# A state-space mixer: silu as one activation, exponentials together, transposes later, decay differences as a biased relu on ACT

## The chip, the cores and the metric

The kernel runs on one core of a Trainium2 chip. The metric is the device time of that core for one launch, in microseconds (us), the median of the runs. The engines are named as in the profile: PE (TensorE, matrix products), PEld (its weight loads), DVE (VectorE), ACT (ScalarE), POOL (GpSimd), and SP, which issues most of the transfers.

## What is computed

The reference is a trunk of two layers over 512 positions of width 1024. The even layer has pooling and chunked attention; the odd layer has a Mamba-2 mixer; each is followed by a mixture of experts. The change touches the odd layer's mixer alone:

```python
zxbcdt = h @ w_in
z, xbc, dt = jnp.split(zxbcdt, [SSM_D_INNER, SSM_D_INNER + SSM_CONV_DIM], axis=-1)
conv = xp[:, 0:s] * conv_w[0]
for tap in range(1, SSM_D_CONV):
    conv = conv + xp[:, tap:tap + s] * conv_w[tap]
xbc = jax.nn.silu(conv + conv_b)
xs, Bm, Cm = jnp.split(xbc, [SSM_D_INNER, SSM_D_INNER + G * N], axis=-1)
...
seg = jnp.exp(jnp.where(tril, a_cs[..., :, None] - a_cs[..., None, :], -jnp.inf))
cb = jnp.einsum('bclgn,bcsgn->bcgls', Cm, Bm)
y_diag = jnp.einsum('bcgls,bcgrls,bcsgrp->bclgrp', cb, seg, x_dt)
...
y = y_diag + y_off + xs * D_skip
g = (y * jax.nn.silu(z)).reshape(b, s, G, SSM_D_INNER // G)
g = g * lax.rsqrt(jnp.mean(g * g, axis=-1, keepdims=True) + EPS)
return (g.reshape(b, s, SSM_D_INNER) * norm_w) @ w_out
```

## The kernel before

The mixer is `odd_mixer` (L1455). It works in 8 head groups g, each with 128 channels of b and of c and two chunks of 128 of x and of z. The positions (512) lie along the free axis, and the scan is done in four position chunks cq of 128. A loop over g = 0 to 8 (L1727) does the projections and most of group g together with the last steps of group g-1.

The steps, with the names of the code and of the trace:

- A projection (`Dense.next`, L436, tiles pdb, pdc, pdx, pdz) is 24 products of 128x512 for 128 channels, since weights and input are split in a high and a low part. There are six per group, in the order b, c, x0, x1, z0, z1. The splits of the weights (L111 on ACT, L112 on DVE or POOL) run ahead.
- `conv` (L1580) reads a projection: a scaled copy with bias on ACT (L1584), three taps on DVE (L1587), Tanh on ACT (L1590), and the product (tanh + 1) times the value on DVE (L1591). The weights are halved beforehand, so this is the silu.
- `cbt` (L1594): c times b per chunk and its mask (cbm), and b transposed (btk).
- `decay` (L1614), for each cq: a row of cumulative decays comes by DMA to all partitions (lb, two buffers); DVE takes the difference to the own decay and its minimum with 0, four heads in turn (L1620, tile ms, three buffers); ACT takes Exp (L1622); POOL (even cq) or DVE (odd cq) multiplies by cbm (L1623).
- `xtok` (L1626): PE transposes x0 and x1 (L1637, pxd); DVE multiplies by the step size (xdt, L1640); POOL makes xw for the first three chunks (L1643).
- `states` (L1645): three products of xw and btk (pst, L1651), summed into prev on ACT and DVE (L1654 to L1659).
- `ymm` (L1661), for each cq: the diagonal products pyd of ms and xdt (L1670) and the products pyo of prev and c (L1674).
- `zgate` (L1677): Tanh of the projection on ACT (L1680), its product on DVE (L1681).
- `assemble` (L1683), for each of the two x chunks: yy and yt on DVE (L1686, L1689), their sum on POOL (L1691), the gate on DVE into gT (L1692), squares on ACT (L1695, L1698) and their sum gsum on POOL.
- `gnorm` (L1701), after every second group for two groups at once: sums over partitions on PE (pgn, L1705), variance gv on DVE (L1708), Ln and Exp on ACT (L1710, L1711), three DVE steps, broadcast to all partitions on POOL (gb, L1718), and gT times it on DVE (L1721).

The short-lived rows (tanh results, yt, squares, gv, gy, gb) share one ring of buffers under the tag "tmp", NTMP of them; a new one waits until the last reader of the buffer's holder is done.

Two other things stand in the same stretch. The modulation of the layer's second half is a product of one vector with a weight matrix of 1024 x 2048, done on DVE as a running sum, one instruction of 128x2048 for each 128 rows (L202 and L204, tile ada); OFILL says how many of these steps are put after each group. And at the end `out_proj` (tiles so) multiplies by w_out.

The order of the code is not the order on the engines. A scheduler orders each engine's instructions at build time by dependences and its own estimates, each engine then runs its list in that order, and waits are put in where they are needed. Exceptions can be pinned by hand.

Of the kernel before, what the change touches and what calls it, by code (L numbers as in the profile page):

```python
# [9 lines left out]
F32 = mybir.dt.float32  # L10
# [10 lines left out]
P = 128  # L21
T = 512
NT = 4
# [35 lines left out]
HEAD = 1  # L59
NTMP = 3  # L60
TAIL = 2
# [15 lines left out]
def trunk_kernel(ctx, tc, x, c, ada_w, ada_b, norm1_w, norm2_w, mix_w_in, pool_w, pool_scale,  # L77
# [1377 lines left out]
    def odd_mixer(layer, prev):  # L1455
        with ExitStack() as es:
# [25 lines left out]
            with ExitStack() as es2:  # L1482
# [94 lines left out]
                def tmp(name):  # L1577
                    return gp.tile([P, T], F32, tag="tmp", name=name, bufs=NTMP)

                def conv(kind, ch, bufs, between=None):  # L1580

                    p = dense.next(between)
                    a = gp.tile([P, T], F32, tag=f"cv{kind}", name=f"cv{kind}{ch}", bufs=bufs)
                    S.activation(a, p, AF.Identity, bias=cb[:, ch:ch + 1], scale=cw[:, 3, ch:ch + 1])  # L1584
                    for tap in (2, 1, 0):
                        sh = 3 - tap
                        V.scalar_tensor_tensor(a[:, sh:], p[:, :T - sh], cw[:, tap, ch:ch + 1], a[:, sh:], op0=ALU.mult,  # L1587
                                               op1=ALU.add)
                    t = tmp(f"cvt{ch}")
                    S.activation(t, a, AF.Tanh)  # L1590
                    V.scalar_tensor_tensor(a, t, 1.0, a, op0=ALU.add, op1=ALU.mult)  # L1591
                    return a
# [21 lines left out]
                def decay(g, cq):  # L1614

                    lb = gp.tile([P, 4, P], F32, tag="lb", name=f"lb{g}{cq}", bufs=2)
                    SP.dma_start(lb, dap(acd, (32 * cq + 4 * g) * P, [[0, P], [1, 4 * P]]))
                    ms = gp.tile([P, 4, P], F32, tag="ms", name=f"ms{g}{cq}", bufs=3)
                    for h in range(4):
                        V.tensor_scalar(ms[:, h, :], lb[:, h, :], acs[:, cq, 4 * g + h:4 * g + h + 1], 0.0,  # L1620
                                        op0=ALU.subtract, op1=ALU.min)
                    S.activation(ms, ms, AF.Exp)  # L1622
                    (V if cq % 2 else GP).tensor_mul(ms, ms, gs[g]["cbm"][:, cq, None, :].to_broadcast([P, 4, P]))  # L1623
                    gs[g]["ms", cq] = ms

# [51 lines left out]
                def zgate(g, q):  # L1677
                    pz = dense.next()
                    z = gs[g]["z", q] = gp.tile([P, T], F32, tag="zt", name=f"zt{g}{q}", bufs=2)
                    S.activation(z, pz, AF.Tanh, scale=0.5)  # L1680
                    V.scalar_tensor_tensor(z, z, 1.0, pz, op0=ALU.add, op1=ALU.mult)  # L1681

                def assemble(g, q):  # L1683
# [7 lines left out]
                    GP.tensor_add(y[:, P:], y[:, P:], t[:, P:])  # L1691
                    V.tensor_mul(gT[2 * g + q], y, d["z", q])  # L1692
                    if q == 0:
# [7 lines left out]
                def gnorm(g0):  # L1701
# [5 lines left out]
                    v = tmp(f"gv{g0}")  # L1707
                    V.tensor_scalar(v, p, 1.0 / 1024, EPS, op0=ALU.mult, op1=ALU.add)  # L1708
                    y = tmp(f"gy{g0}")
                    S.activation(y, v, AF.Ln)  # L1710
                    S.activation(y, y, AF.Exp, scale=-0.5)  # L1711
                    t = tmp(f"gt{g0}")
                    V.tensor_mul(t, y, y)
                    V.scalar_tensor_tensor(t, t, -0.25, v, op0=ALU.mult, op1=ALU.mult)
                    V.scalar_tensor_tensor(y, t, 0.75, y, op0=ALU.add, op1=ALU.mult)
                    for q in range(2):
# [10 lines left out]
                for g in range(G + 1):  # L1727
# [8 lines left out]
                    if g:  # L1736
                        ymm(g - 1, 0)
                        ymm(g - 1, 1)
                        decay(g - 1, 3)
                    if d is not None:  # L1740
                        d["c"] = conv("c", 24 + g, 2)
                    if g:
                        ymm(g - 1, 2)
                        ymm(g - 1, 3)
                    if d is not None:
                        d["x", 0] = conv("x", 2 * g, 3)
                    if g:
                        assemble(g - 1, 0)
                        assemble(g - 1, 1)
                    if d is not None:  # L1750
                        d["x", 1] = conv("x", 2 * g + 1, 3)
                        if g == 0:
                            next(dt)
                            zgate(g, 0)
                            next(dt)
                        cbt(g)
                        if g:
                            zgate(g, 0)
                        decay(g, 0)
                        xtok(g)  # L1760
                        zgate(g, 1)
                        decay(g, 1)
                        states(g)
                        decay(g, 2)
                        for _ in range(OFILL[g]):
                            if fill:
                                next(fill.pop(0), None)
                    if g == G - 1:
# [3 lines left out]
                        moe.weights(W8)  # L1772
                    if g and g % 2 == 0:
                        gnorm(g - 2)
            moe.open(xd, "left")
# [68 lines left out]
```

## Time and profile before

| | us |
|---|---|
| median of 3 runs | 1093.95 |
| the runs | 1093.01, 1093.95, 2492.22 |
| the profiled execution | 1094.89 |
| its span in the profile | 1093.0 |

| engine | busy in the whole span | instructions |
|---|---|---|
| PE | 985.5 us (90%) | 5700 |
| DVE | 715.6 us (65%) | 1607 |
| ACT | 388.7 us (36%) | 753 |
| POOL | 282.9 us (26%) | 324 |

The mixer's groups 1 to 7 lie between 477.5 and 814.7 us of the span: b of group 1 starts at 477.5, b of group 7 at 762.7, the output projection at 814.7. A busy share is an average over stages with different limits, so for a change in one stage the rows of that stage are read: what each engine does in it, and which wait of PE ends last. In the rows, `x` counts instructions, `out<-in` names tiles, and `<-` in brackets names what ended an idle time.

### The profile page before, as it was taken

Reading aid. Unit: us, or ns where it says so; the run is one execution under the profiler, and the core shown is the slowest. Engines: PE = TensorE matmul, PEld = TensorE weight load, DVE = VectorE, ACT = ScalarE, POOL = GpSimd, SP = SyncE. Lnnn points to the kernel's source line nnn. Section 1 sums busy time; section 2 is a strip of 40 time slices with the busy share of each in tenths; the row PEclk is TensorE's granted clock in tenths of the full one; section 3 lists DMA queues with packets and bytes.
Section 4 is the critical chain, followed back from the end, with each engine's and each line's share of the span. In section 5 each row is a group of like instructions: output and inputs, shape, how many; then the busy total and the mean of one; then the engine's idle time right before and its main releaser. Section 6 shows DMA issues by size and latency. Waiting matters only on the chain. (4 is left out here: it accounts for less than half of the span.)

```text
span 1093.0 us, 15960 instructions
## 1 busy us (share of the span) xinstructions
PE 985.5 (90%) x5700; PEld 726.6 (66%) x5700; DVE 715.6 (65%) x1607; ACT 388.7 (36%) x753; POOL 282.9 (26%) x324
## 2 busy tenths in 40 slices
PE   5799998896999997997999899799989998899994
PEld 4576555685666666786877777687767877565653
DVE  3523434445657767868988799977886555555874
ACT  4334533333223334324244333443424235223242
POOL 3002111114321045123241434324141005231134
PEclk9899999997999999998999999899989998899998
DMA  8689867796899989445742475454444844799987
GB/s 318 229 276 314 289 227 283 275 350 203 286 407 413 407 165 346 110 127 183 263 146 88 140 219 191 126 164 102 140 135 151 330 151 181 238 406 413 410 274 184
DMA packets 137841, 263.88 MB, mean 241 GB/s; under 512 B 17556, under 2 KB 79976, under 8 KB 132633
## 3 DMA queue, kind: packets, MB, share of 16 engines
q1 hardware_dynamic: 126760, 235.36, 61.4%
q0 software_dynamic: 8928, 20.97, 7.3%
q10 hardware_dynamic: 2064, 6.42, 1.5%
q8 instruction: 49, 0.80, 0.3%
q14 instruction: 40, 0.32, 0.1%
HBM read 254.15 MB, written 20.11 MB: 251 GB/s over the span
## 5 line engine op out<-in xcount | busy, mean ns | idle before, releaser
L1063 PE MATMUL ph<-w,xT 128*64 128x256 f32 (+1 forms) x1152 | 132.1, 373 | 2.5 <-DVE xT L1047 2.3
L1063 PEld LDWEIGHTS ph<-w,xT 128*64 128x64 f32 x1152 | 86.5, 139 | 53.6 <-ACT xT L1049 9.5
L1030 POOL DMA_INDIRECT xg<-xnd,toks x32 | 32.2, 1007 | 150.3 <-PE pxt L1042 113.8
L1084 PE MATMUL pyy<-w,hidT 128*64 128x512 f32 x272 | 65.9, 605 | 2.2 <-ACT hidT L1076 2.2
L1065 ACT ACTIVATE th<-ph 128x128 f32<-128x128 f32 x34 | 9.4, 277 | 154.8 <-PE pht L1074 136.7
L1049 ACT ACTIVATE xT<-pxt,mc 128x128 f32<-128x128 f32 x136 | 51.1, 456 | 17.8 <-PE pxt L1042 12.3
L1089 DVE SCALAR_TENSOR_TENSOR y<-pyy,wsl,gate 128x512 f32<-128x512 f32 x68 | 48.0, 744 | 5.9 <-DMA yd<-y 4.3
L1042 PE MATMUL pxt<-ident,xg 128*128 128x128 f32 x272 | 37.9, 284 | 15.4 <-DVEq L1415 9.0
L1047 DVE TENSOR_SCALAR xT<-pxt,mc 128x128 f32<-128x128 f32 x136 | 46.6, 405 | 1.4 <-PE pxt L1042 1.4
L1066 DVE SCALAR_TENSOR_TENSOR th<-th,ph 128x128 f32<-128x128 f32 x34 | 9.8, 287 | 57.2 <-ACT th L1065 57.2
L1042 PEld LDWEIGHTS pxt<-ident,xg 128*128 128x128 f32 x272 | 34.5, 194 | 15.9 <-issue 15.5
L1115 DVE TENSOR_TENSOR x<-x,pyc 128x512 f32<-128x512 f32 x48 | 30.4, 682 | 20.9 <-DMA x<-yd,row 11.4
L1620 DVE TENSOR_SCALAR ms<-lb,acs 128x128 f32<-128x128 f32 x128 | 37.8, 335 | 6.5 <-DMA lb<-acd 4.2
L1587 DVE SCALAR_TENSOR_TENSOR cvx<-pdx,cw,cvx 128x511 f32<-128x511 f32 (+2 forms) x48 | 35.4, 738 | 8.2 <-ACT cvx L1584 8.1
L1210 POOL DMA_INDIRECT x<-yd,row x16 | 25.5, 1592 | 48.9 <-issue 24.1
L1623 POOL TENSOR_TENSOR ms<-ms,cbm 128x512 f32<-128x512 f32 x16 | 31.9, 1999 | 17.9 <-ACT ms L1622 16.0
L202 DVE SCALAR_TENSOR_TENSOR ada<-ada,ccol,ada 128x2048 f32<-128x2048 f32 x14 | 34.9, 2496 | 0.1
L1084 PEld LDWEIGHTS pyy<-w,hidT 128*64 128x64 f32 x272 | 16.5, 136 | 26.0 <-issue 19.4
L492 DVE TENSOR_TENSOR sor<-sor,gate 128x1024 f32<-128x1024 f32 x16 | 19.9, 1246 | 19.4 <-DMA sor<-in_ssm_w_out_dram 19.3
L1670 PE MATMUL pyd<-ms,xdt 128*64 128x128 f32 x256 | 20.2, 291 | 9.5 <-DVE ms L1623 9.5
L1622 ACT ACTIVATE ms<-ms 128x512 f32<-128x512 f32 x32 | 19.8, 623 | 24.6 <-DVE ms L1620 24.5
L1637 PE MATMUL pxd<-ident,cvx 128*128 128x128 f32 x64 | 11.6, 316 | 17.2 <-DVE cvx L1591 17.2
(1079 smaller groups left out, 2770.2 us busy)
## 6 DMA issues: line engine op xcount, KB each, us to landing
w<-in_moe_w_dram SPq DMA_DIRECT2D x192, 512.0 KB
ada<-in_ada_w_dram SPq DMA_DIRECT2D x40, 1024.0 KB
yd<-y SPq DMA_DIRECT2D x22, 512.0 KB
ada<-in_ada_w_dram SPq DMA_DIRECT2D x16, 512.0 KB
wx<-in_ssm_w_in_dram SPq DMA_DIRECT2D x16, 512.0 KB
wz<-in_ssm_w_in_dram SPq DMA_DIRECT2D x16, 512.0 KB
lb<-acd SPq DMA_DIRECT2D x32, 256.0 KB
sor<-in_ssm_w_out_dram SPq DMA_DIRECT2D x16, 512.0 KB
```

The costliest lines, as they stand in the source:

```text
L202: a = eng.scalar_tensor_tensor(ws[k], ws[k], ccol[:, k:k + 1], ws[k - 1], op0=ALU.mult, op1=ALU.add)
L1030: d = GP.indirect_dma_start(out=xg, out_offset=None, in_=xnd[:, :], in_offset=bass.IndirectOffsetOnAxis(ap=idx, axis=0), bounds_check=T - ...
L1042: PE.transpose(p[:, q, :], xv[:, 4 * hf + q, :], ident)
L1047: V.tensor_scalar(xT[:, k, :], p[:, q, :], a, b, op0=ALU.mult, op1=ALU.add)
L1049: S.activation(xT[:, k, :], p[:, q, :], AF.Identity, bias=b, scale=a)
L1063: PE.matmul(ph[64 * j:64 * j + 64, n:n + h, :], xT[:, k, 64 * j:64 * j + 64], w13[n][:, :, k, :], start=k == 0, stop=k == KD - 1, skip_gro ...
L1084: PE.matmul(py[64 * j:64 * j + 64], hT[:, 64 * j:64 * j + 64], w2[:, s], start=True, stop=True, skip_group_check=True)
L1089: V.scalar_tensor_tensor(y[:, s], py, self.wsl[:, slot:slot + 1], self.gate2[:, s], op0=ALU.mult, op1=ALU.mult)
L1115: V.tensor_add(xst["x"][i][:, s], xst["x"][i][:, s], p)
L1587: V.scalar_tensor_tensor(a[:, sh:], p[:, :T - sh], cw[:, tap, ch:ch + 1], a[:, sh:], op0=ALU.mult, op1=ALU.add)
L1620: V.tensor_scalar(ms[:, h, :], lb[:, h, :], acs[:, cq, 4 * g + h:4 * g + h + 1], 0.0, op0=ALU.subtract, op1=ALU.min)
L1623: (V if cq % 2 else GP).tensor_mul(ms, ms, gs[g]["cbm"][:, cq, None, :].to_broadcast([P, 4, P]))
```

## The change

- The silu of the convolutions and of the gate becomes one Silu activation on ACT; the Tanh and the DVE product go. Group 0's four convolutions and its first gate keep the Tanh, so that group's first gated row carries a factor 0.5 and the variance's constant changes from 1/1024 to 1/256.
- The decay's difference is taken on ACT: four Relu with scale -1 and the own decay as bias, then Exp with scale -1. All four cq of a group come together in `exps`, between the convolutions of x0 and x1; the mask product is apart, in `masked`. ms has four buffers, the tmp ring two.
- `in_order` fixes the order of all Silu, of the decays' Exp, and of the norm's Ln and Exp on ACT, without a wait.
- `xtok` stands after both gates instead of between them; `states` of group g stands after b of group g+1; the diagonal products of the first two chunks come after c, those of the others after x0.
- `gnorm` stands inside `exps` of groups 3, 5 and 7 (for groups 0 and 1, 2 and 3, 4 and 5) and after the loop for 6 and 7. The DVE step that refines its root no longer halves the result.

```diff
@@ -57,7 +57,7 @@
-NTMP = 3
+NTMP = 2
@@ -1577,6 +1577,14 @@
+                acts = []
+
+                def in_order(a):
+
+                    if acts:
+                        tc.add_manual_dep(a.ins, acts[-1].ins.name, NOSYNC, reason="in_order")
+                    acts.append(a)
...
@@ -1586,6 +1594,9 @@
                         sh = 3 - tap
                         V.scalar_tensor_tensor(a[:, sh:], p[:, :T - sh], cw[:, tap, ch:ch + 1], a[:, sh:], op0=ALU.mult,
                                                op1=ALU.add)
+                    if acts:
+                        in_order(S.activation(a, a, AF.Silu, scale=2.0))
+                        return a
                     t = tmp(f"cvt{ch}")
                     S.activation(t, a, AF.Tanh)
                     V.scalar_tensor_tensor(a, t, 1.0, a, op0=ALU.add, op1=ALU.mult)
@@ -1615,13 +1626,23 @@
                     lb = gp.tile([P, 4, P], F32, tag="lb", name=f"lb{g}{cq}", bufs=2)
                     SP.dma_start(lb, dap(acd, (32 * cq + 4 * g) * P, [[0, P], [1, 4 * P]]))
-                    ms = gp.tile([P, 4, P], F32, tag="ms", name=f"ms{g}{cq}", bufs=3)
+                    ms = gs[g]["ms", cq] = gp.tile([P, 4, P], F32, tag="ms", name=f"ms{g}{cq}", bufs=4)
                     for h in range(4):
-                        V.tensor_scalar(ms[:, h, :], lb[:, h, :], acs[:, cq, 4 * g + h:4 * g + h + 1], 0.0,
-                                        op0=ALU.subtract, op1=ALU.min)
-                    S.activation(ms, ms, AF.Exp)
+                        S.activation(ms[:, h, :], lb[:, h, :], AF.Relu, scale=-1.0,
+                                     bias=acs[:, cq, 4 * g + h:4 * g + h + 1])
+                    in_order(S.activation(ms, ms, AF.Exp, scale=-1.0))
+
+                def exps(g):
+
+                    if g > 2 and g % 2:
+                        gnorm(g - 3)
+                    for cq in range(NT):
+                        decay(g, cq)
+
+                def masked(g, cq):
+
+                    ms = gs[g]["ms", cq]
                     (V if cq % 2 else GP).tensor_mul(ms, ms, gs[g]["cbm"][:, cq, None, :].to_broadcast([P, 4, P]))
-                    gs[g]["ms", cq] = ms
...
@@ -1677,6 +1698,9 @@
                 def zgate(g, q):
                     pz = dense.next()
                     z = gs[g]["z", q] = gp.tile([P, T], F32, tag="zt", name=f"zt{g}{q}", bufs=2)
+                    if acts:
+                        in_order(S.activation(z, pz, AF.Silu))
+                        return
                     S.activation(z, pz, AF.Tanh, scale=0.5)
                     V.scalar_tensor_tensor(z, z, 1.0, pz, op0=ALU.add, op1=ALU.mult)
...
-                    V.tensor_mul(gT[2 * g + q], y, d["z", q])
+                    if g + q:
+                        V.tensor_mul(gT[2 * g + q], y, d["z", q])
+                    else:
+                        V.scalar_tensor_tensor(gT[2 * g + q], y, 0.5, d["z", q], op0=ALU.mult, op1=ALU.mult)
...
-                    V.tensor_scalar(v, p, 1.0 / 1024, EPS, op0=ALU.mult, op1=ALU.add)
+                    V.tensor_scalar(v, p, 1.0 / 256, EPS, op0=ALU.mult, op1=ALU.add)
                     y = tmp(f"gy{g0}")
-                    S.activation(y, v, AF.Ln)
-                    S.activation(y, y, AF.Exp, scale=-0.5)
-                    t = tmp(f"gt{g0}")
-                    V.tensor_mul(t, y, y)
-                    V.scalar_tensor_tensor(t, t, -0.25, v, op0=ALU.mult, op1=ALU.mult)
-                    V.scalar_tensor_tensor(y, t, 0.75, y, op0=ALU.add, op1=ALU.mult)
+                    in_order(S.activation(y, v, AF.Ln))
+                    in_order(S.activation(y, y, AF.Exp, scale=-0.5))
+                    V.scalar_tensor_tensor(v, v, -0.5, y, op0=ALU.mult, op1=ALU.mult)
+                    V.tensor_mul(v, v, y)
+                    V.scalar_tensor_tensor(y, v, 1.5, y, op0=ALU.add, op1=ALU.mult)
@@ -1734,34 +1760,37 @@
                     if g:
-                        ymm(g - 1, 0)
-                        ymm(g - 1, 1)
-                        decay(g - 1, 3)
+                        states(g - 1)
                     if d is not None:
                         d["c"] = conv("c", 24 + g, 2)
                     if g:
+                        ymm(g - 1, 0)
+                        ymm(g - 1, 1)
+                    if d is not None:
+                        d["x", 0] = conv("x", 2 * g, 3)
+                    if g:
                         ymm(g - 1, 2)
                         ymm(g - 1, 3)
+                    if d is not None and g:
+                        exps(g)
                     if d is not None:
-                        d["x", 0] = conv("x", 2 * g, 3)
+                        d["x", 1] = conv("x", 2 * g + 1, 3)
                     if g:
                         assemble(g - 1, 0)
                         assemble(g - 1, 1)
                     if d is not None:
-                        d["x", 1] = conv("x", 2 * g + 1, 3)
                         if g == 0:
                             next(dt)
                             zgate(g, 0)
                             next(dt)
+                            exps(g)
                         cbt(g)
                         if g:
                             zgate(g, 0)
-                        decay(g, 0)
+                        zgate(g, 1)
                         xtok(g)
-                        zgate(g, 1)
-                        decay(g, 1)
-                        states(g)
-                        decay(g, 2)
+                        for cq in range(NT):
+                            masked(g, cq)
                         for _ in range(OFILL[g]):
                             if fill:
...
-                    if g and g % 2 == 0:
-                        gnorm(g - 2)
+                    if g == G:
+                        gnorm(G - 2)
```

The change moves instructions on every engine. On DVE, between groups 3 and 4, this stood before (names: xdt3 is group 3's, ada12 the modulation's running sum, adab its result):

```order
L1640 TENSOR_TENSOR xdt3_6081<-pxd31_6092,dtk_4656 128x256 x2
L1681 SCALAR_TENSOR_TENSOR zt31_6131<-zt31_6131,pdz31_6106 128x512
L1656 TENSOR_TENSOR prev3_6143<-prev3_6143,cdec_4659 128x256
L215 TENSOR_TENSOR adab11_5063<-pada11_6164,adab11_5063 128x512
L1659 TENSOR_TENSOR prev3_6143<-prev3_6143,pst31_6147 128x256
L204 TENSOR_SCALAR ada120_6185<-ada120_6185,ccol_94 128x2048
```

and this stands there now:

```order
L1661 TENSOR_TENSOR xdt3_6106<-pxd31_6117,dtk_4656 128x256 x2
L215 TENSOR_TENSOR adab11_5059<-pada11_6129,adab11_5059 128x512
L204 TENSOR_SCALAR ada120_6150<-ada120_6150,ccol_94 128x2048
L202 SCALAR_TENSOR_TENSOR ada121_6152<-ada121_6152,ccol_94,ada120_6150 128x2048
L202 SCALAR_TENSOR_TENSOR ada122_6154<-ada122_6154,ccol_94,ada121_6152 128x2048
L1595 SCALAR_TENSOR_TENSOR cvb20_6193<-pdb4_6168,cw_124,cvb20_6193 128x511
L112 TENSOR_TENSOR x41l_6214<-wx41_6162,x41h_6213 128x1024
L1595 SCALAR_TENSOR_TENSOR cvb20_6193<-pdb4_6168,cw_124,cvb20_6193 128x510
L202 SCALAR_TENSOR_TENSOR ada123_6157<-ada123_6157,ccol_94,ada122_6154 128x2048
L1595 SCALAR_TENSOR_TENSOR cvb20_6193<-pdb4_6168,cw_124,cvb20_6193 128x509
L202 SCALAR_TENSOR_TENSOR ada124_6160<-ada124_6160,ccol_94,ada123_6157 128x2048
L1747 SCALAR_TENSOR_TENSOR gT0_5077<-gT0_5077,vcol_123,gb01_5934 128x512 x2
L1713 TENSOR_TENSOR yt20_6009<-pyo20_5858,eb2_5656 128x384
L1713 TENSOR_TENSOR yt21_6017<-pyo21_5859,eb2_5656 128x384
```

Group 2's yt and the last products of the norm of groups 0 and 1 have moved behind group 3's xdt, five modulation products and the taps of group 4's b.

On POOL, around group 3's xw, before (yy2 is group 2's sum, ms3 group 3's mask product):

```order
L1691 TENSOR_TENSOR yy20_5966<-yy20_5966,yt20_5968 128x384
L1691 TENSOR_TENSOR yy21_5974<-yy21_5974,yt21_5976 128x384
L1699 TENSOR_TENSOR gsum2_5972<-gsum2_5972,sq2_5980 128x512
L1623 TENSOR_TENSOR ms30_6074<-ms30_6074,cbm3_6030 128x512
L1623 TENSOR_TENSOR ms32_6157<-ms32_6157,cbm3_6030 128x512
L1643 TENSOR_TENSOR xw3_6082<-xdt3_6081,dec_4658 128x256 x3
```

and now (gb01 is a broadcast row of the norm):

```order
L1744 ISA gb01_5934<-gy0_5924 128x512
L1664 ISA
L1664 TENSOR_TENSOR xw3_6107<-xdt3_6106,dec_4658 128x256
L1715 TENSOR_TENSOR yy20_6007<-yy20_6007,yt20_6009 128x384
L1715 TENSOR_TENSOR yy21_6015<-yy21_6015,yt21_6017 128x384
L1664 TENSOR_TENSOR xw3_6107<-xdt3_6106,dec_4658 128x256 x2
```

The two adds of group 2 now stand between the first xw of group 3 and the other two.

On ACT, in group 3, before (cvx6 and cvx7 are its x0 and x1, cvt the tanh, b4h a weight split):

```order
L1584 ACTIVATE cvx6_5958<-pdx30_5933,cb_130,cw_124 128x512
L1622 ACTIVATE ms30_6074<-ms30_6074 128x512
L1622 ACTIVATE ms31_6136<-ms31_6136 128x512
L1590 ACTIVATE cvt6_5963<-cvx6_5958 128x512
L111 ACTIVATE b4h_6040<-wb4_5983 128x1024
L1584 ACTIVATE cvx7_6014<-pdx31_5989,cb_130,cw_124 128x512
```

and now:

```order
L1631 ACTIVATE ms33_5964<-lb33_5962,acs_4657 128x128 x4
L1598 ACTIVATE cvx6_5901<-cvx6_5901 128x512
L1737 ACT_TABLE_LOAD
L1737 ACTIVATE gy0_5924<-gv0_5922 128x512
L111 ACTIVATE b4h_6042<-wb4_5970 128x1024
L1738 ACT_TABLE_LOAD
L1738 ACTIVATE gy0_5924<-gy0_5924 128x512
L1633 ACTIVATE ms30_5940<-ms30_5940 128x512
L1633 ACTIVATE ms31_5948<-ms31_5948 128x512
L1633 ACTIVATE ms32_5956<-ms32_5956 128x512
L1633 ACTIVATE ms33_5964<-ms33_5964 128x512
L1592 ACTIVATE cvx7_6001<-pdx31_5976,cb_130,cw_124 128x512
```

The norm's Ln and Exp, with their table loads, and all four Exp stand between the Silu of x0 and the scaled copy of x1. ACT's list has 21 table loads in the whole program, 9 before.

## Rows read from the trace of the kernel before

**Rows 1.** The span cut at starts of groups: us, busy (x) by engine, PEclk, DMA, GB/s.

```profile
core 0: us, PE busy (x) PEld busy (x) DVE busy (x) ACT busy (x) POOL busy (x), PEclk, DMA share, GB/s
...
621.00:664.90 43.90, 41.81 (x222) 33.15 (x218) 43.37 (x61) 16.38 (x24) 16.33 (x13) 1.00 0.68 207
...
762.70:814.70 52.00, 47.50 (x254) 37.56 (x252) 45.09 (x78) 20.81 (x30) 14.47 (x11) 0.93 0.41 131
sum 337.20, PE 310.47 PEld 246.57 DVE 293.95 ACT 130.15 POOL 116.60; mean PE 44.35 PEld 35.22 DVE 41.99 ACT 18.59 POOL 16.66
```

**Rows 2.** PE's waits, 477 to 815: what for, us in total, times, longest.

```profile
PE pxd L1637 <- DVE cvx L1591: 17.2, 7, 4.1
PE pyd L1670 <- DVE ms L1623: 9.5, 4, 4.4
```

**Rows 3.** PE in order of time: start, us, line, operation, tiles, [idle before].

```profile
656.76 0.88 PE L1637 MATMUL pxd<-ident,cvx 128*128 128x128 f32 x6 [2.09 <-DVE cvx L1591]
...
663.89 1.08 PE L1705 MATMUL pgn<-gsum,ones 128*64 128x512 f32 x4
...
755.81 0.40 PE L452 MATMUL pdz<-sh_hi,z61l 128*128 128x512 f32 x1
...
757.18 0.39 PE L452 MATMUL pdz<-sh_hi,z61l 128*128 128x512 f32 x1
...
758.80 1.06 PE L212 MATMUL pada<-ada,ones 128*32 128x512 f32 x8
759.79 1.98 PE L249 MATMUL plb<-wr,mc 128*128 128x40 f32 x16
```

**Rows 4.** The stretch after PE's longest wait, columns as in rows 1.

```profile
686.70:693.50 6.80, 6.21 (x20) 4.82 (x21) 4.83 (x9) 1.98 (x3) 0.14 (x1) 0.50 0.58 163
```

**Rows 5.** DVE's groups, 477 to 815, by form: busy us, mean ns | idle before.

```profile
L1620 DVE TENSOR_SCALAR ms<-lb,acs 128x128 f32<-128x128 f32 x128 | 37.8, 335 | 6.5 <-DMA lb<-acd 4.2 <-PE pyd L1670 2.3
L202 DVE SCALAR_TENSOR_TENSOR ada<-ada,ccol,ada 128x2048 f32<-128x2048 f32 x14 | 34.9, 2496 | 0.1
L1591 DVE SCALAR_TENSOR_TENSOR cvx<-cvt,cvx 128x512 f32<-128x512 f32 x14 | 15.7, 1121 | 0.8 <-ACT cvt L1590 0.8
...
L1587 DVE SCALAR_TENSOR_TENSOR cvx<-pdx,cw,cvx 128x511 f32<-128x511 f32 x14 | 10.4, 743 | 8.1 <-ACT cvx L1584 8.1
...
L1681 DVE SCALAR_TENSOR_TENSOR zt<-zt,pdz 128x512 f32<-128x512 f32 x15 | 10.2, 681 | 18.0 <-ACT zt L1680 18.0
L1640 DVE TENSOR_TENSOR xdt<-pxd,dtk 128x256 f32<-128x256 f32 x28 | 9.9, 411 | 0.0
L1721 DVE SCALAR_TENSOR_TENSOR gT<-gT,vcol,gb 128x512 f32<-128x512 f32 x12 | 8.8, 792 | 1.6 <-POOL gb L1718 1.6
L1689 DVE TENSOR_TENSOR yt<-pyo,eb 128x384 f32<-128x384 f32 x14 | 7.1, 545 | 0.0
L1591 DVE SCALAR_TENSOR_TENSOR cvc<-cvt,cvc 128x512 f32<-128x512 f32 x7 | 6.7, 953 | 0.6 <-ACT cvt L1590 0.6
...
L1591 DVE SCALAR_TENSOR_TENSOR cvb<-cvt,cvb 128x512 f32<-128x512 f32 x7 | 4.8, 683 | 0.2 <-ACT cvt L1590 0.2
...
L204 DVE TENSOR_SCALAR ada<-ada,ccol 128x2048 f32<-128x2048 f32 x2 | 2.6, 1280 | 0.0
```

**Rows 6.** ACT in order of time, two places: start, us, line, operation, tiles.

```profile
294.00 1.50 ACT L1049 ACTIVATE xT<-pxt,mc 128x128 f32<-128x128 f32 x4
...
576.05 1.28 ACT L1710 ACT_TABLE_LOAD   x1 [2.71 <-DVE gv L1708]
577.35 0.63 ACT L1710 ACTIVATE gy<-gv 128x512 f32<-128x512 f32 x1
578.00 1.28 ACT L1711 ACT_TABLE_LOAD   x1
...
579.83 1.04 ACT L111 ACTIVATE x31h<-wx 128x1024 fp32r<-128x1024 f32 x1
```

**Rows 7.** POOL's groups, 477 to 815: busy us, mean ns | idle before.

```profile
L1691 POOL TENSOR_TENSOR yy<-yy,yt 128x384 f32<-128x384 f32 x14 | 17.0, 1238 | 16.6 <-DVE yt L1689 16.6
L1643 POOL TENSOR_TENSOR xw<-xdt,dec 128x256 f32<-128x256 f32 x21 | 16.2, 800 | 13.7 <-DVE xdt L1640 13.7
```

## The prediction

> **What bounds the kernel now.** I read four views, in this order. First the span cut at the starts of the groups [rows 1]: in the seven groups from 477.5 to 814.7 us TensorE (PE) is busy 310.5 of 337.2 us, VectorE (DVE) 294.0, ACT 130.2, POOL 116.6. PE is the bound, DVE is close behind it, ACT has room. Then what PE waits for there [rows 2]: 17.2 us for DVE's last step on the x chunks, ahead of the transposes, and 9.5 us for DVE's mask product, ahead of the diagonal products. So PE's idle time is mostly a wait for DVE; the longest of these are 4.1 and 4.4 us. Then PE in order of time [rows 3], for what a group consists of. Last the granted clock [rows 4]: 0.50 (the 1.2 GHz level) in the 6.8 us that follow the wait of 4.4, so 3.4 us lost behind it.
>
> The changed part thus has a floor. The group from 621.0 ran at a granted clock of 1.00 and lasted 43.9 us; without its wait of 2.09 and the norm's products, 1.08, a group needs 40.7. The six groups from 477.5 to 762.7 last 285.2 us, and PE is busy 263.0 of them (310.47 less the last group's 47.50). Their floor is 6 x 40.7, plus the norm's products 3 x 1.08, the modulation's 2 x 1.06 and the router's 1.98 [rows 3]: 251.5. The other 33.7 are 22.2 idle and 11.5 lost at half clock: the most that these six can give back. The last group (52.0) is taken apart below.
>
> **What leaves and what comes.** From DVE go [rows 5] the 128 differences at 0.335, 37.8 us; the 28 tanh products of the convolutions, 15.7 + 6.7 + 4.8 = 27.2; the gate's 15, 10.2. That is 75 of 294: DVE falls to some 219 of 337 us, 65%. The waits of [rows 2] are then no longer DVE's: the transposes stand one dense projection later (24 products started 0.23 apart, six steps from 755.81 to 757.18 [rows 3]: 5.5 us), and the mask products find all their exponentials done early in the group. I take both waits as gone.
>
> To ACT come 112 relus in these seven groups. No Relu with a bias is in the trace; the bounds are DVE's 0.335 for the same shape and 0.63 for an activation four times as wide. I take 0.375, since four activations of 128x128 with operands per partition take 1.50 [rows 6]: 42 us. The order has 21 table loads against 9 in the program, 11 of the 12 more in this stretch. A load takes 1.28, and the next activation starts 1.30 after it [rows 6]: 14.3 us. For Silu I take the 0.63 of any 128x512 activation there, as for the Tanh it replaces. ACT goes to 130 + 42 + 14 = 186 us, 55%: the work moves to an engine that has room, and costs nothing as long as no one waits for ACT.
>
> The Trainium skill ("ScalarE: Activation LUTs", section "Rules for kernel authors") says to keep relu on VectorE instead of ScalarE. Per instruction the rows bear it out mildly (0.335 against 0.375). By the rule the move would be a loss, but 87% of DVE against 39% of ACT in [rows 1] decides it here.
>
> **ACT's chain.** The change fixes the order of Silu, Exp and Ln on ACT, so a late one holds all behind it. In a norm group (3, 5, 7), counted from b's first product: PE needs 3 x 5.5 for b, c, x0, and about 4.9 of a group's 7.7 us of small products (40.7 less six projections) stand among and right behind them, so the diagonal products of the group before are done near 21.4. They free the buffers of the last eight relus: 24.4. I take 25.4, a microsecond more for DVE's variance step. Then Silu 0.63, load 1.30, Ln 0.63, a weight split 1.04, load 1.30, Exp 0.63, four Exps 2.5, x1's bias step 0.6, DVE's three taps 2.2, load and Silu 1.9: 38.1. PE reaches the transposes near 40.0: the norm's products 1.08 and three projections after 21.4, and 1.0 for the group's other products. Slack 1.9. Plain groups lack Ln, its Exp, one load and the variance step: slack about 5. No wait, but little to spare.
>
> **The new wait.** The temporaries get two buffers instead of three. In a norm group the variance and the root take both, then the two broadcast rows, so yt of the group before can't be written until gT has been multiplied. The orders show yt behind that on DVE, and POOL's second and third xw behind the two adds that need yt. PE's second states product needs that xw. So DVE, POOL and PE stand in one line. On SP only the decay rows' loads move, to an earlier place; nothing that PE waits for is behind them.
>
> Between groups 3 and 4, from the end of the first half of the transposes, DVE has four xdt (4 x 0.411), an add that I take as a tap (0.74), the modulation's first product 1.28 and four more at 2.50, b's taps 2.2, a split (taken as ACT's 1.04), two gT (2 x 0.792) and the first yt 0.55: 19.0 [rows 5]. Of these 0.8 lies beside the second half of the transposes: 18.2. POOL adds twice and makes one xw, 2 x 1.24 + 0.80 = 3.3 [rows 7]: 21.5. PE has meanwhile 1.06 of the modulation, b's 5.5 and about 0.5 of the first states product: 7.1. Wait 14.4, and 3.4 of half clock as in [rows 4]: 17.8. Bounds: nothing, as in rival A below, and 17.8 + 3 if both xw are late.
>
> Between groups 5 and 6 there is no modulation. From b's start: 5.5, bias step 0.6, taps 2.2, gT 1.6, yt 0.55, POOL 3.3: 13.8 against PE's 6.0. Wait 7.8 and 3.4: 11.2, with the like bounds.
>
> The six groups: 251.5 + 17.8 + 11.2 = 280.5 against 285.2, so 4.7 us less. DVE's relief is given back at two places.
>
> **The tail.** In the last group the transposes come after both gates, and no projection is left to lie over what follows: xdt and xw (0.41 + 3 x 0.80 = 2.8), the state sums (about 2), and yt and gT in DVE's queue (about 2). The granted clock of 0.93 in [rows 1] means 3.6 us lost of 52.0; I count two thirds of it, 2.4, as lost on busy time. PE's 47.5 less 2.4 is 45.1; with 7 idle and 3.4 of half clock behind it, 55.5 against 52.0: 3.5 more. Bounds: 4 less, if the output projection's first products cover the line, to 10 more.
>
> **Sum.** -4.7 + 3.5 = -1.2. The profiled execution took 1094.89 (its span 1093.0 and 1.9 around it), 0.9 above the median of 1093.95: 1093.7 for it, 1092.8 on the median.
>
> **Rivals.** A: yt's line costs nothing. If the adds and xw reach their turn before PE does, the 29.0 of the two places stay won: 1063.8. For it: POOL is busy 116.6 of 337.2, a third [rows 1]. Against it: in the fixed order of DVE five modulation products, 11.3 us, stand ahead of yt.
>
> B, on the slower side: ACT's chain becomes the bound. The relus of the third and fourth chunk wait for the diagonal products of the group before, and Silu of x0, Ln, the Exps and x1's steps all stand behind them. PE waits from 1.9 us of lateness in norm groups, from 5 in plain ones. At 6 us late it is (4.1 + 3.4) x 3 + 1 x 4 = 26.5 more: 1119. For it: a chain in fixed order with 17 loads takes over what DVE's free choice did. Against it: ACT at 55%.
>
> C: a table load costs more than its row. If ACT had to run empty around each and lost 1.28 again, the three of a norm group's chain make 3.8, less 1.9 of slack, plus 3.4 of half clock: 5.3 x 3 = 16 more, 1109. Against it: the load at 578.00 starts 0.02 after the end of the Ln before it [rows 6].
>
> The Trainium skill ("ScalarE: Activation LUTs", section "What ACT_TABLE_LOAD costs") puts a switch at about 1283 ns of load and 1380 ns of drain. The first is what the rows show; the second is not seen there, and by it the time would be C's.
>
> **How the numbers follow.** A measurement of this kernel can tell about 2%, 21.9 us, from no change: faster is below 1072, slower above 1116. Forecast 0.58, A 0.17, B 0.16, C 0.09. A falls under faster, nearly all of B under slower, the rest within 2%: 0.17, 0.68, 0.15. The range reaches to A and most of the way to B, 1065 to 1115; the tail's bounds (7.5 less and 6.5 more than I take) and partial waits at the two places lie inside it. The forecast's own range is 1080 to 1102.
>
> **What would show it.** Right: no wait on DVE's conv step ahead of the transposes and none on the mask products; waits of PE of about 14 and 8 us for POOL's xw behind groups 3 and 5; relus of 0.35 to 0.40 us; 21 loads at 1.28 with the next activation 1.30 behind; plain groups of 41 to 42 us; a last group 3 to 4 us longer than 52. Wrong: no wait on xw (A), a wait of PE on ACT's Silu in every norm group (B), gaps on ACT ahead of its loads (C).

## The result and the profile after

The changed kernel takes 1131.17 us (median of 4, 1128.06 to 1134.62), 1.034 times the kernel before (95% interval 1.0315 to 1.0366): slower by 37 us, beyond the range's 1115. The run of 2492.22 us in the table of the kernel before is a slow one and is not part of the comparison. The profiled execution has a span of 1132.8 us, against 1093.0.

The span cut at the starts of its groups (columns as in [rows 1]):

```profile
477.40:521.50 44.10, 40.81 (x216) 33.21 (x214) 33.83 (x40) 31.48 (x63) 18.34 (x12) 1.00 0.70 205
521.50:569.50 48.00, 43.21 (x215) 34.53 (x213) 32.56 (x38) 24.45 (x43) 19.45 (x10) 0.93 0.58 188
569.50:613.10 43.60, 42.95 (x229) 33.60 (x227) 24.25 (x35) 24.70 (x43) 10.60 (x8) 1.00 0.36 105
613.10:679.10 66.00, 43.46 (x218) 34.47 (x214) 48.87 (x51) 24.98 (x45) 22.42 (x16) 0.82 0.63 202
679.10:721.50 42.40, 41.76 (x220) 33.39 (x218) 23.52 (x33) 24.52 (x43) 10.04 (x8) 1.00 0.37 101
721.50:790.80 69.30, 46.68 (x240) 36.67 (x238) 31.48 (x46) 25.67 (x47) 21.30 (x17) 0.83 0.30 83
790.80:855.30 64.50, 51.67 (x272) 39.32 (x271) 42.28 (x57) 26.46 (x47) 16.08 (x15) 0.89 0.37 123
sum 377.90, PE 310.54 PEld 245.18 DVE 236.79 ACT 182.26 POOL 118.24; mean PE 44.36 PEld 35.03 DVE 33.83 ACT 26.04 POOL 16.89
```

Against [rows 1], DVE's 294.0 are 236.8 and ACT's 130.2 are 182.3, so the work moved as meant; PE's busy time is the same. Groups 3 and 5 run at 43.6 and 42.4, full clock. The stretches behind them take 66.0 and 69.3, the last 64.5. Before, group 4 took 43.9 and the last 52.0 [rows 1], and group 6 this:

```profile
714.40:762.70 48.30, 46.34 (x243) 36.37 (x241) 36.59 (x61) 17.25 (x26) 17.46 (x12) 0.96 0.47 129
```

So these three are 55.6 us longer than before, the other four together 14.9 shorter, and the seven groups lose 40.7. PE's waits in them (as in [rows 2]):

```profile
PE pst L1672 <- POOL xw L1664: 61.1, 8, 20.9
PE pxd L1658 <- ACT cvx L1598: 4.2, 4, 1.7
PE pdx L449 <- DVE cvb L1595: 2.1, 1, 2.1
```

The longest two, with the product behind the first of them, in order of time (as in [rows 3]):

```profile
639.68 1.22 PE L1672 MATMUL pst<-xw,btk 128*128 128x256 f32 x2 [20.83 <-POOL xw L1664]
642.61 2.24 PE L1672 MATMUL pst<-xw,btk 128*128 128x256 f32 x4 [1.71 <-POOL xw L1664]
...
748.08 1.22 PE L1672 MATMUL pst<-xw,btk 128*128 128x256 f32 x2 [20.91 <-POOL xw L1664]
```

The waits of [rows 2] on DVE are gone, and one on POOL's xw has come, 61.1 us. POOL in order of time behind group 3 (start, us, what, [idle before]):

```profile
611.59 0.80 POOL L1744 PARTITION_BROADCAST gb<-gy  x1 [5.71 <-issue]
619.73 4.22 POOL L112 TENSOR_TENSOR x40l<-wx,x40h 128x1024 fp32r<-128x1024 f32 x1 [7.33 <-ACT x41h L111]
630.86 0.80 POOL L1744 PARTITION_BROADCAST gb<-gy  x1 [6.92 <-issue]
639.02 0.60 POOL L1664 TENSOR_TENSOR xw<-xdt,dec 128x256 f32<-128x256 f32 x1 [7.36 <-issue]
639.60 1.93 POOL L1715 TENSOR_TENSOR yy<-yy,yt 128x384 f32<-128x384 f32 x2
641.50 2.08 POOL L1664 TENSOR_TENSOR xw<-xdt,dec 128x256 f32<-128x256 f32 x2
```

POOL has no work queued here, it stands still: 5.71, 7.33, 6.92 and 7.36 us, before and after each partition broadcast, mostly with "issue", for which the profile shows no cause. The input of the first xw had long been there, from DVE:

```profile
613.76 1.41 DVE L1661 TENSOR_TENSOR xdt<-pxd,dtk 128x256 f32<-128x256 f32 x4
```

One of these places stood unread in a fence of the section on the change: a row without a tile, L1664 ISA, between gb01 and the first xw. I take such a row to load the code (the library) that the next operation belongs to, and call the place a change of library. That code is loaded is a reading: the trace shows the idle time alone, and no more DMA packets (137840 in the whole kernel, 137841 before). In the trace POOL goes from a broadcast to another operation or back 12 times, in the kernel before 8 times, and each time it is idle for 5.7 us or more. In the kernel before, the two broadcasts of a norm stand together; here, in the norms of groups 3 and 5, a weight split comes between them, so these two norms have four changes instead of two, and xw behind the last. In group 7 the pair stays together, with xw right behind it.

The Trainium skill ("GPSIMD Engine Reference", section "2.1 Instruction dispatch") says that the first call to a freshly loaded GpSimd kernel pays some 6 us of loading that no instruction of the profile shows. The trace agrees in size (5.7 to 7.4 us where it gives "issue"), and has it at each change, in both directions.

### The profile page after: what moved, and what is told of

Read it like the earlier page. It is cut to its first block, busy times and chain, and to the rows that moved or that the text cites. A ratio compares the mean times of both kernels' runs of the same rounds, so it can differ in the third digit from the quotient of the medians.

```text
span 1132.8 us, 15982 instructions
## 1 busy us (share of the span) xinstructions
PE 985.9 (87%) x5700; PEld 727.5 (64%) x5700; DVE 653.6 (58%) x1436; ACT 440.9 (39%) x893; POOL 281.8 (25%) x324
## 2 busy tenths in 40 slices
DMA packets 137840, 263.87 MB, mean 233 GB/s; under 512 B 17556, under 2 KB 79976, under 8 KB 132633
## 5 line engine op out<-in xcount | busy, mean ns | idle before, releaser
L1672 PE MATMUL pst<-xw,btk 128*128 128x256 f32 x48 | 19.4, 540 | 61.1 <-POOL xw L1664 61.1
L1672 PEld LDWEIGHTS pst<-xw,btk 128*128 128x128 f32 x48 | 10.6, 248 | 68.0 <-POOL xw L1664 67.1
L1631 ACT ACTIVATE ms<-lb,acs 128x128 f32<-128x128 f32 x128 | 39.4, 390 | 5.4 <-DMA lb<-acd 5.4
L1645 POOL TENSOR_TENSOR ms<-ms,cbm 128x512 f32<-128x512 f32 x16 | 26.1, 1647 | 38.9 <-DVE cbm L1618 31.7
L1107 PE MATMUL pyc<-yh,yot 128*128 128x512 f32 x96 | 28.2, 427 | 3.8 <-DVE yot L1097 3.8
```

The lines of the kernel that those rows point to most:

```text
L1107: PE.matmul(p, part[2][:, i * P:(i + 1) * P], part[hf][:, q * 512:(q + 1) * 512], start=not sums and n + q == 0, stop=stop and n == len(pa ...
L1631: S.activation(ms[:, h, :], lb[:, h, :], AF.Relu, scale=-1.0, bias=acs[:, cq, 4 * g + h:4 * g + h + 1])
```

## The experiments

Each time is the median of four or more runs, in us; in brackets stand its ratio to the kernel before, run on the same chip, and the 95% interval of the ratio. The edits are shown in excerpts. Theory L is that PE waits for POOL's changes of library; the rivals are the prediction's own reading or parts of it.

**1. No broadcasts on POOL.** PE makes the rows, read from PSUM.

```diff
-                        b = tmp(f"gb{g0}{q}")
-                        GP.partition_broadcast(b, y[64 * q:64 * q + 1, :])
+                        b = ps(name=f"gb{g0}{q}")
+                        PE.matmul(b, ones[64 * q:64 * q + 1, :], y[64 * q:64 * q + 1, :], start=True, stop=True)
```

> The changed kernel with the norm's two broadcast rows made by PE (a product of one row of ones with the root's row, read from PSUM) instead of POOL's partition broadcast, so they are also out of the ring of temporaries. Theory L (each change of POOL between a partition broadcast and its other operations costs 6 to 7 us in which POOL does nothing, and in the changed kernel four such changes per norm stand ahead of the weighted inputs xw that PE waits for): the waits of PE on xw behind groups 3, 5 and 7 (20.8, 20.9, 9.5 us) fall under 3 us each and the half clock behind them goes; 51 + 10 us less, about 4 us of PE products more: some 1075. Rival Q (the prediction's own: the wait is yt's queue on DVE behind the two buffers, worth 14.4 and 7.8, the rest unexplained): the queue goes too as the rows leave the ring, but the unexplained 20 us and more stay: about 1100.

1121.83 (ratio 1.028, 1.0235 to 1.033). PE's waits:

```profile
PE gb L1744 <- DVE gy L1741: 34.1, 4, 9.1
PE pst L1672 <- POOL xw L1664: 7.0, 5, 1.9
PE pgn L1732 <- POOL gsum L1726: 5.6, 1, 5.6
```

The wait on xw fell from 61.1 to 7.0, no single one above 1.9, as L said. Neither time came, 1075 or 1100: PE's list has the new product right behind the norm's sums, so PE now waited up to 9.1 us for the root that ACT and DVE had yet to make. One wait took the other's place.

**2. The same, with the rows copied by ACT into the ring of two**, so that the ring stays as tight.

```diff
+                        pb = ps(name=f"pgb{g0}{q}")
+                        PE.matmul(pb, ones[64 * q:64 * q + 1, :], y[64 * q:64 * q + 1, :], start=True, stop=True)
                         b = tmp(f"gb{g0}{q}")
-                        GP.partition_broadcast(b, y[64 * q:64 * q + 1, :])
+                        S.activation(b, pb, AF.Copy)
```

> The changed kernel with the broadcast rows made by PE and then copied by ACT into the ring of two temporaries, so the ring is as tight as in the changed kernel and only POOL's broadcasts are gone. L: as with PE's broadcasts alone, plus the copies on ACT and some microseconds for the ring: 1075 to 1085; waits on xw under 4 us. Q: the ring is what holds yt, so waits of about 14 and 8 us on xw stay and the time is 1105 or more.

1120.83 (1.0265, 1.0227 to 1.0302): a time of the rival's, but with L's waits, 7.0 in all on xw and the same 9.1 on the root. With two buffers and no broadcast on POOL in these groups, the waits of 14 and 8 us that the prediction had put down to yt's queue are not there. This does not test that queue as the changed kernel has it, since here yt stands ahead of xdt in DVE's list (from 602.27 against 619.88).

**3. Three buffers, broadcasts on POOL.**

```diff
-NTMP = 2
+NTMP = 3
-                cdec = gp.tile([P, NT, 32], F32, name="cdec")
+                cdec = gp.tile([P, 2, 32], F32, name="cdec")
```

> The changed kernel with three buffers in the ring (space made by keeping two of four chunks of the chunk decays, the only ones used), so that the two broadcasts of a norm stand together and yt goes ahead of the transposes' products on DVE. L: two of four changes of POOL per norm go, two stay: after the pair ends near 0.8 us later than the first did, 7 us of change, one weight split 2.4, two adds 2.4 and xw 0.8 bring xw some 13 us behind the pair where PE wants it some 6 behind: waits of about 7 to 8 us instead of 21, 1100 to 1105 in all. Q: yt is free, all the waits go: 1070 or less.

1103.88 (1.0107, 1.0071 to 1.0143), as L had it; three long waits on xw, 8.4, 7.6 and 11.3. POOL:

```profile
608.15 1.48 POOL L1744 PARTITION_BROADCAST gb<-gy  x2 [5.66 <-ACT cvx L1598]
618.54 2.33 POOL L112 TENSOR_TENSOR x40l<-wx,x40h 128x1024 fp32r<-128x1024 f32 x1 [8.91 <-DMA modd<-adab]
620.84 1.93 POOL L1715 TENSOR_TENSOR yy<-yy,yt 128x384 f32<-128x384 f32 x2
622.74 2.65 POOL L1664 TENSOR_TENSOR xw<-xdt,dec 128x256 f32<-128x256 f32 x3
```

The pair stands together, and one stand-still is left between it and xw. So the third buffer gives back 27 of the 37 us. Two things change at once: there are fewer stand-stills, and yt stands ahead of xdt on DVE again.

**4. The kernel before, with the pair split.** A tiny product is forced between the two broadcasts of each norm.

```diff
-                        GP.partition_broadcast(b, y[64 * q:64 * q + 1, :])
+                        if q:
+                            one = GP.tensor_mul(tiny, pidx, pidx)
...
+                            cast.append(GP.partition_broadcast(b, y[64 * q:64 * q + 1, :]))
...
+                        else:
+                            cast = [GP.partition_broadcast(b, y[64 * q:64 * q + 1, :])]
```

> The kernel before with one tiny product of POOL (one element per partition) forced between the two broadcasts of each norm; nothing else is added and nothing reordered by hand. L: two more changes of POOL per norm, 14 us on POOL each time, and DVE's second pair of gT products, which stand in its list some places behind the first, wait for it and hold up what is behind: 15 to 45 us slower than before, 1110 to 1140. Q: a tiny product costs under 1 us: within 3 us of before.

1104.61 (1.0123, 1.0081 to 1.0166), 12 us slower for four products of 0.2 us: the rival falls, but L had 15 at least. POOL stood still as in the changed kernel:

```profile
577.64 0.81 POOL L1725 PARTITION_BROADCAST gb<-gy  x1 [7.32 <-DVE gy L1716]
585.92 0.18 POOL L1720 TENSOR_TENSOR tiny<-pidx 128x1 f32<-128x1 f32 x1 [7.47 <-issue]
592.42 0.80 POOL L1722 PARTITION_BROADCAST gb<-gy  x1 [6.31 <-ACT ms L1623]
600.39 2.54 POOL L112 TENSOR_TENSOR z31l<-wz,z31h 128x1024 fp32r<-128x1024 f32 x1 [7.17 <-issue]
```

Behind the pair stand a weight split and, 11 us later, xw. In the profiled run, the fastest of the four (1099.03), groups 1 to 7 last 338.0 us, as before (337.2), and the 4 us that the span is longer come behind the last norm, beside the output projection. So the stand-stills themselves are shown here, and that in these groups, with nothing behind them that PE needs soon, they cost next to nothing; where the other 8 us of the median went is not shown.

**5 to 8. The change without the library.** PE's broadcasts come behind the first gate, the last norm's stay on POOL.

```diff
                             zgate(g, 0)
+                        if g > 2 and g % 2:
+                            gspread(g - 3)
                         zgate(g, 1)
```

> The changed kernel, broadcasts of the first three norms by PE as in the earlier run, but PE's broadcast products written behind the first gate's projection instead of right behind the norm's sums (there PE waited 9.1 us three times for the root); the last norm, beside the output projection, keeps POOL's broadcast. Theory L (POOL's changes of library were what PE waited for, and nothing else of the change costs much): no wait over 2 us is left in groups 1 to 6, so against that run 3 x (9.1 + 3.4) + 7.0 + some half clock less: 1072 to 1082, some 15 us faster than before. Rival R (the queue of yt and ACT's fixed order cost as much as the change gives, as in the prediction's sum): 1090 or more.

> The same with three buffers in the ring of temporaries. L: the ring no longer matters once POOL's broadcasts are gone: within 5 us of the run with two. R: yt is freed, 10 us or more faster than with two.

> The kernel before with the first three norms' broadcasts by PE, written behind the next group's c, the last by POOL. L: in the kernel before the changes of library lie beside idle time of POOL (25.6 us of its idle time stands ahead of the six broadcasts) and cost PE little: 1088 to 1098, so what the late broadcasts gain belongs to the changed kernel alone. Rival S (the library costs any kernel of this form the same): 1075 to 1080, 15 us faster than before.

> The changed kernel with late broadcasts by PE and two buffers, but the decays' differences on DVE as before (subtract and minimum, Exp with scale 1). DVE takes 112 x 0.335 = 38 us back in the groups, ACT loses about 42. L: neither engine bounds in the groups, so within 6 us of the run with the relus on ACT. Rival D (DVE was the bound that the change removed, and the relus are half of the 75 us): 10 to 15 us slower than it.

Two buffers: 1090.62 (0.9965, 0.9915 to 1.0015; the four runs from 1081.68 to 1094.73). Three: 1077.78 (0.9858, 0.9832 to 0.9885). The kernel before with late broadcasts: 1093.09 (1.000, 0.9967 to 1.0032). Relus back on DVE, two buffers: 1097.12 (1.0036, 1.0004 to 1.0068).

Taking the broadcasts off POOL and placing their products late is worth 41 us to the changed kernel, and nothing to the kernel before: as the two are ordered, the changes of library cost the changed kernel alone. L's time for two buffers (1072 to 1082) was missed all the same, and the rival's (1090 or more) came: without the changes of library the changed kernel with two buffers is no faster than the kernel before. L's sentence that the ring no longer matters fell too: the third buffer is worth some 13 us here. Through what is not shown: PE's waits in the two profiles differ by 7 us (24.3 and 17.1 in all, none over 3.6), and yt stands ahead of xdt in both. The relus on ACT are 6.5 us faster than on DVE, between the two expectations (6, and 10 to 15), with intervals that overlap; nothing hangs on it.

With three buffers xw was still waited for, 11.4 us in all:

```profile
606.80 2.40 POOL L112 TENSOR_TENSOR x40l<-wx,x40h 128x1024 fp32r<-128x1024 f32 x1 [7.48 <-ACT x40h L111]
609.16 6.83 POOL L1664 TENSOR_TENSOR xw<-xdt,dec 128x256 f32<-128x256 f32 x3
```

Three xw took 6.83 us here, beside DVE's modulation products, and 2.73 in the next group (658.08), where DVE had none.

**9. Two buffers in the kernel before**, with the norm's formula in place.

> The kernel before with a ring of two temporaries and the norm's formula worked in place (without which two do not do); silu, decays and order of the code as before. Theory L (two buffers hurt the changed kernel by splitting the pair of POOL's broadcasts and by holding yt behind the norm): the pair stays together here in POOL's list, so no more changes of library; the tanh rows of the convolutions share the ring, so some holding is left: 1093 to 1105. Rival T (two buffers alone cost what the changed kernel lost): 1115 or more.

1096.78 (1.0023, 1.0004 to 1.0042), as L had it: the pair stays together on POOL, and two buffers cost 2 to 3 us. So two buffers alone do not cost what the changed kernel lost; with run 3, it is the order that the scheduler made with them there.

**10 to 12. With three buffers: xw on DVE; the transposes back between the gates; xw on DVE with POOL's broadcasts.**

```diff
-                                GP.tensor_mul(xw[:, cq], xdt[:, cq], dec[:, cq, hs, None].to_broadcast([P, 4, 64]))
+                                V.tensor_mul(xw[:, cq], xdt[:, cq], dec[:, cq, hs, None].to_broadcast([P, 4, 64]))
```

```diff
+                        xtok(g)
                         zgate(g, 1)
-                        xtok(g)
```

> The changed kernel with late broadcasts by PE and three temporaries, xw made by DVE instead of POOL (21 products in the groups). PE waits 11.4 us on POOL's xw in the run with POOL; beside DVE's modulation products POOL took 6.83 us for three xw where it takes 1.8 alone. L: the waits fall to 4 or less and some half clock goes: 1066 to 1073. Rival: DVE's queue, with the modulation products in it, is as late as POOL: 1076 or more.

> The changed kernel with late broadcasts by PE and three temporaries, the transposes and their products written between the two gates again, as in the kernel before. In the run that this undoes, x1's Silu is done 1 to 8 us before the transposes. L: with 5.5 us less, PE waits 3 to 5 us for the Silu in norm groups, and less or nothing in the others; but xw gets 5.5 us more ahead of the states' products, which takes away most of the 11.4 us of that wait: 1074 to 1084. Rival: the transposes' place is what the change gains by, and it loses 15 us or more: 1092 or more.

> The changed kernel with three temporaries and POOL's broadcasts where the change put them, with xw made by DVE. Theory L in its sharper form (a change of POOL's library costs PE only what POOL's next product that PE waits for is late): the changes stay, two per norm, but xw no longer stands behind them, so the waits of 8.4, 7.6 and 11.3 us that the run with three temporaries had on xw go, and the half clock behind them: 1070 to 1080, near the run with broadcasts by PE and xw on DVE (1071.9). Rival (the changes hold up something else as well, POOL's mask products or DVE through the broadcast rows): 1088 or more.

xw on DVE: 1071.93 (0.9799, 0.9781 to 0.9817), as L had it, the fastest, 2% below the kernel before. Its groups, the first six at full clock:

```profile
608.60:650.30 41.70, 40.58 (x216) 33.11 (x213) 40.25 (x43) 22.25 (x41) 18.17 (x9) 1.00 0.91 273
650.30:693.60 43.30, 42.92 (x223) 33.69 (x222) 32.57 (x45) 25.97 (x45) 11.80 (x7) 1.00 0.50 151
```

Transposes in the old place: 1086.28 (0.9911, 0.9877 to 0.9945), slower than in the new one by 8.5 us, or 6 by the ratios, between the two expectations (1074 to 1084, and 1092 or more); the wait on xw is gone, and PE waited for the Silu in every group instead:

```profile
PE pxd L1658 <- ACT cvx L1598: 16.6, 7, 3.3
```

POOL's broadcasts with xw on DVE: 1079.97 (0.9877, 0.982 to 0.9933), where L had it. POOL stands still as long as ever:

```profile
601.54 1.48 POOL L1744 PARTITION_BROADCAST gb<-gy  x2 [5.89 <-PE pxd L1658]
611.78 3.33 POOL L112 TENSOR_TENSOR x40l<-wx,x40h 128x1024 fp32r<-128x1024 f32 x1 [8.76 <-DMA modd<-adab]
```

and PE's longest wait on xw is 4.7. Against run 3 (1103.88) that is 24 us, for moving 24 small products off POOL. What the stand-still costs PE depends on what stands behind it on POOL, and here that was xw.

## Why the prediction was wrong

**What held.** ACT was put at 186 us; it is 182.3. A relu with its bias takes 0.39 where 0.375 was taken. A table load costs 1.28, and the next activation starts 1.30 after it, so rival C is out:

```profile
595.48 1.28 ACT L1737 ACT_TABLE_LOAD   x1
596.78 0.63 ACT L1737 ACTIVATE gy<-gv 128x512 f32<-128x512 f32 x1
...
610.50 0.63 ACT L1598 ACTIVATE cvx<-cvx 128x512 f32<-128x512 f32 x1
```

ACT's chain ended 41.6 us after b of group 3 (569.5), where 38.1 was reckoned against 40.0 wanted; PE waited for it 4.2 us in all, so rival B is out too, by little. The waits of [rows 2] on DVE went, and xw was named as the new wait, behind the groups where it came. That the place was right is partly luck: the broadcast that holds up yt is also what makes POOL stand still.

**What held less.** DVE's busy time fell by 57.2 us, not by 75; the mask products of ms, for one, took 19.8 us instead of 14.2. The 63% of 377.9 come near the forecast 65% only because the span grew.

**The step that failed** is POOL's share in the sum of the new wait. It was taken as "2 x 1.24 + 0.80 = 3.3", as if POOL were ready whenever yt came, and the time around each broadcast was put at nothing without a reason. With DVE's 18.2 this made waits of 14.4 and 7.8, before the second states product. Measured are 20.83 and 20.91 before the first one, which needs no yt, and only 1.71 behind each. The equal size shows what the sum had wrong, since one place has DVE's modulation products and the other has none. DVE behind group 5:

```profile
729.21 2.31 DVE L1595 SCALAR_TENSOR_TENSOR cvb<-pdb,cw,cvb 128x511 f32<-128x511 f32 x3
740.27 1.42 DVE L1747 SCALAR_TENSOR_TENSOR gT<-gT,vcol,gb 128x512 f32<-128x512 f32 x2 [8.76 <-POOL gb L1744]
741.60 1.02 DVE L1713 TENSOR_TENSOR yt<-pyo,eb 128x384 f32<-128x384 f32 x2
```

DVE was idle for 8.76 us, waiting for POOL's second broadcast; behind group 3, where the modulation kept it busy, for 0.84. At both places yt was done 5 us and more before POOL was ready for its adds (634.04 against 639.60, 742.62 against 748.00). So DVE's queue was not what PE waited for. POOL's four changes, 27.3 us at group 3 (5.71 + 7.33 + 6.92 + 7.36), were left out. Runs 1 and 2 take them away, run 3 leaves fewer, and run 12 leaves fewer and takes xw off POOL: of the 61.1 us on xw there remain 7.0, 7.0, 31.2 and 7.0.

The line through yt was not far off, it only ended second. An estimate from these rows: with POOL ready, the second xw would have been done near 636 and 736.5, and PE, free at 619.5 and 727.8, would have waited some 16 and 9 us. No run shows this by itself, since in runs 1 to 3, 5 and 6 the scheduler put yt ahead of xdt.

Of the 41.9 us by which the seven groups missed the sum (40.7 more instead of 1.2 less), 23.0 lie at the two places (25.9 and 26.0 with the 1.71 and the half clock, for 17.8 and 11.2), 9.0 in the tail, and 9.9 in the rest of the six groups, which did not come down to the floor that was reckoned. Most of these lie in group 2, which has no broadcast: it took 48.0, with waits of 3.26 and 1.53 on xw and 3.4 of half clock.

**The tail** was put at 3.5 more than 52.0 and is 12.5 more: the same change of library stands ahead of its xw, for which PE waited 9.47 us (7 idle in all were reckoned, and the half clock).

**The half clock** was right: 3.4 us behind each long wait, at a granted clock of 0.50 (the 1.2 GHz level) after PE had been idle for some 20 us (columns as in [rows 4]).

```profile
639.70:646.50 6.80, 5.09 (x11) 3.31 (x12) 5.85 (x6) 3.04 (x6) 6.80 (x7) 0.50 0.05 14
748.10:754.90 6.80, 5.09 (x11) 3.31 (x12) 3.76 (x5) 2.93 (x6) 5.14 (x5) 0.50 0.00 0
```

**Rival A** (yt's line costs nothing, 1063.8) was reached by no run. The nearest are 1077.78 with late broadcasts and three buffers, and 1071.93 with xw on DVE as well. What keeps them 8 to 14 us above it is only partly shown: small waits are left, 11.4 us on xw in the first.

## What to carry to other kernels

Read every row of an engine's order, also those without a tile: on POOL such a row stood for 6 to 7 us of idle time. So POOL's broadcasts should stand together, with no other operation between them and nothing urgent behind. When two lines meet at a wait, reckon both to their end, also that of an engine with much idle time. What the missing buffer cost here was paid in good part where the scheduler then split such a pair, not where the buffer is used. A product that replaces a wait must stand where its input is ready, or PE waits for that instead.

## What the runs showed that was not expected

POOL's stand-still around each partition broadcast, 5.7 to 8.7 us where the profile names no cause, also around a product of 0.18 us. And POOL's xw beside DVE's products of 128x2048, in run 6: three in 6.83 us at 609.16, 2.73 in the next group; DVE's first product there took 2.35 us, where it took 1.28 in [rows 5]. The Trainium skill ("GPSIMD Engine Reference", section "1. Specifications") says that GpSimd's access to SBUF is shared with VectorE, with contention when DVE's instruction has two SBUF inputs or runs in a mode with two ports; the rows fit this, but no run here separates it from other causes.
